# FFN-in with tokens stationary, and two pairs of its blocks per layer as seven products of quadrants

## The chip, the cores and the metric

The kernel runs on one core of a Trainium2 chip. The metric is device microseconds from the start to the end of one execution, smaller is better. The engines of a core are TensorE (PE, with its weight load PEld), VectorE (DVE), ScalarE (ACT), GpSimd (POOL) and SyncE (SP); each runs its own list of instructions in order, and waits in it for semaphores. Transfers are issued from a queue of SP or of GpSimd and run on sixteen DMA engines that all queues share.

## The reference

Two layers, 256 tokens of 1,024 features, everything in 32-bit floats. A layer is a mixer (gated linear attention beside grouped-query attention), then the FFN, then an embedding step:

```python
u = rms_norm(h, g_mix_pre);  h = h + rms_norm(mixed @ w_out, g_mix_post)     # the mixer
gate, up = jnp.split(rms_norm(h, g_ffn_pre) @ w_ffn_in, 2, axis=-1)          # w_ffn_in: 1024 x 5632
h = h + rms_norm((jax.nn.silu(gate) * up) @ w_ffn_out, g_ffn_post)           # w_ffn_out: 2816 x 1024
h = h + rms_norm(jax.nn.sigmoid(h @ w_ple_gate) * (p_i @ w_ple_proj), g_ple_post)
```

The change is in the second line. The hidden width 2,816 is cut into eleven blocks of 256; block b takes 256 gate columns and the 256 up columns that belong to them.

## The kernel before

Every product of 32-bit numbers is made from three products of TensorE in its fp32r type: each operand is split into a rounded high part and the rest, and high x high, high x low and low x high are summed (`mm3`, line 87). The split of one piece is a cast on ScalarE and a subtraction on VectorE (`split`, line 99).

**Weights.** `plan` (line 162) lists, in the order of use, units of 1,024 KB: for FFN-in a unit is 512 rows of one block's 512 columns (`unit_gate_up`), so a block has two, kh = 0 and 1. `Stream` (line 177) takes them through three stages. `load` issues a unit's transfers on SP's queue into one of two `raw` buffers. `fill` splits a unit in two pieces, k = 0, 1 and k = 2, 3, into a pair of buffers `wh` and `wl`, of which there are four, and then issues the next load. `take` hands a split unit to TensorE's code; `done` says that it has been used, and lets `fill` go on. So up to four units are split ahead of their use, the one in use among them.

**Tokens.** `Split` (line 258) holds a matrix in transposed form, features on the partitions and tokens along the free axis, as high and low parts. `u2` is the normed input of the FFN, `hid` its hidden values. `Task` (line 229) is a generator of small work, transposes above all, that `tick` moves on after every few products, so that TensorE meets it some products later; `need` runs it to its end.

**FFN-in** (lines 1027 to 1052). Blocks 0 and 1 have the tokens stationary (`amode`, line 383): 128 tokens by 128 features are loaded, 512 columns of weights move, and the result has tokens on the partitions. One half of the tokens (hf) goes first, since `u2` comes half by half. The gated result is transposed on TensorE (line 291) into `hid`. Blocks 2 to 10 have the weights stationary (`wmode`, line 392): 128 x 128 weights are loaded, 256 tokens move, the result is already transposed, and goes into `hid` after silu and the product with up. FFN-out (from line 1059) reads `hid`.

The order on each engine is fixed when the program is compiled, from the order of the code, priorities and estimated times. Buffers come from pools: `big` has nine of 8 KB a partition, `mid` ten of 4 KB, `acc` and `aux` eight PSUM banks. SCRATCH (1,024 bytes a partition) is what is set aside in SBUF for the descriptors of transfers that GpSimd's queue issues; the kernel before issues none.

Of the kernel before, what the change touches and what calls it, by code (L numbers as in the profile page):

```python
# [9 lines left out]
F32 = mybir.dt.float32  # L10
# [6 lines left out]
P = 128  # L17
T = 256
# [21 lines left out]
def trunk_kernel(ctx: ExitStack, tc: tile.TileContext, a: dict, out: bass.AP):  # L40
# [21 lines left out]
    def nm(s):  # L62
        uid[0] += 1
        return f"{s}_{part[0]}_{uid[0]}"
# [98 lines left out]
    for l in range(DEPTH):  # L163
        w = a["w_in"][l]
        plan += [unit_rows(w, n, C_RA, C_RA + 1056, 2 if l + n == 0 else 1) for n in range(4)]
        for c0 in (C_AK, C_GQ, C_GK, C_GV, C_GV + 512, C_GG, C_GG + 512, C_GA, C_GA + 512, C_GB, C_GB + 512):
            plan += [unit(w, kh, c0) for kh in range(2)]
        for j in range(2):
            for wo in (a["w_o_gla"][l], a["w_o_attn"][l]):
                plan += [unit(wo, kh, j * 512) for kh in range(2)]  # L170
        plan += [unit(a["w_out"][l], kh, j * 512) for kh in range(2) for j in range(2)]
        plan += [unit_rows(a["w_ple_proj"][l], 0)]
        plan += [unit_gate_up(a["w_ffn_in"][l], kh, b) for b in range(NBLK) for kh in range(2)]
        plan += [unit_rows(a["w_ffn_out"][l], n) for n in range(NBLK)]
        plan += [unit(a["w_ple_gate"][l], kh, j * 512) for kh in range(2) for j in range(2)]

    class Stream:


        def __init__(self, depth):  # L180
            self.depth, self.n, self.held, self.raws, self.ready, self.open = depth, 0, 0, [], [], False

        def load(self, between=lambda: None):

            if self.n == len(plan):
                return
            raw = rawp.tile([P, UNIT], F32, tag="raw", name=nm("raw"))
            moves = plan[self.n](raw)
            for dst, src in moves:
                if self.open:  # L190
                    nc.sync.dma_start(dst, src)
                else:
                    on("dma", nc.sync.dma_start, dst, src)
                between()
            self.raws.append((raw, sum(math.prod(dst.shape[1:]) for dst, _ in moves)))
            self.n += 1

        def pieces(self):

            raw, n = self.raws.pop(0)  # L200
# [4 lines left out]
            return [(wh[:, c], wl[:, c], raw[:, c]) for c in (slice(0, n // 2), slice(n // 2, n))]  # L205

        def fill(self):
# [50 lines left out]
    class Split:  # L258


        def __init__(self):
            self.h, self.l = (big(F32R).rearrange("p (k t) -> p k t", t=T) for _ in range(2))
            self.makers = {0: [], 1: []}

        def need(self, hf, k=None):

# [7 lines left out]

        def put(self, src, k, n, t0, tn):

            i = (slice(None), slice(k, k + n), slice(t0, t0 + tn))
            split(self.h[i], self.l[i], src.rearrange("p (k t) -> p k t", t=tn))

        def tok(self, k, hf):  # L280
            s = slice(hf * P, (hf + 1) * P)
            return self.h[:, k, s], self.l[:, k, s]

        def all(self, k):
            return self.h[:, k, :], self.l[:, k, :]

    def transpose_in(sp, src, k, n, hf):

# [103 lines left out]
    def wmode(os_, sp, k0, w, first, last):  # L392
# [9 lines left out]
        for f in range(4):  # L402
# [6 lines left out]
                )  # L409
            tick()  # L410

    def project_t(sp):
# [113 lines left out]
    def turned(hf, k, n):  # L526

        ps = aux()
        for i in range(n):
            on("pe", nc.tensor.transpose, ps[:, i * P : (i + 1) * P], xn[hf][:, (k + i) * P : (k + i + 1) * P], ident)  # L530
        i = (slice(None), slice(k, k + n), slice(hf * P, (hf + 1) * P))
        split_here(uT.h[i], uT.l[i], ps[:, : n * P].rearrange("p (k t) -> p k t", t=P))

    def start():
        square(0, 0)
# [40 lines left out]
    for l in range(DEPTH):  # L576
# [448 lines left out]


        part[0] = f"{l}ffnin"
        hid = [Split() for _ in range(3)]
        us = [[ws.take() for _ in range(2)] for _ in range(2)]
        for hf in range(2):  # L1030
            for b in range(2):
                o = acc()
                for kh in range(2):
                    amode(o, u2, hf, kh * 4, us[b][kh], kh == 0, kh == 1)
                    if hf == 1:
                        ws.done()
                sg = t512()
                nc.scalar.activation(sg[:, 0:256], o[:, 0:256], AF.Silu)
                vmul(sg[:, 0:256], o[:, 256:512], sg[:, 0:256])


                def turn(sg=sg, b=b, hf=hf):
                    yield WAIT_FFN
                    transpose_in(hid[0], sg[:, 0:256], b * 2, 2, hf)

                hid[0].makers[hf].append(Task(turn(), part[0]))
# [17 lines left out]
        def out_step(n, hf, w):  # L1064
            wh, wl = (t[:, :2048].rearrange("p (k c) -> p k c", c=512) for t in w)
            for kk in range(2):
                k = 2 * n + kk
                hid[k // 8].need(hf)
                for j in range(2):
                    mm3(  # L1070
                        o[hf][j], hid[k // 8].tok(k % 8, hf), (wh[:, 2 * kk + j, :], wl[:, 2 * kk + j, :]),
                        k == 0, k == 2 * NBLK - 1,
                    )
                tick()
# [95 lines left out]
```

## Time and profile before

| | |
|---|---|
| median of 3 runs | 953.19 us (952.98 to 954.38) |
| profiled execution | 953.27 us |
| its span, first to last instruction | 951.6 us |
| TensorE busy | 938.7 us, 99% |
| VectorE, ScalarE, GpSimd busy | 612.7, 508.4, 80.9 us |
| granted clock of TensorE | 0.998 |
| read from HBM | 167.41 MB, 177 GB/s over the span |

A row of a group reads: line, engine, operation, output <- inputs by their buffers' names, partitions x elements, count; then busy us and mean ns of one; then the time its engine was idle just before, and what ended that. The number behind a buffer's name is the layer, the text behind it the part of the program in which the buffer was handed out. Products overlap in TensorE, so the mean duration of one is longer than the time from one to the next. In the chain of waits a row is start, length, and what ran (x is the count); "issue" is time in which the engine waited for nothing that the profile shows. A DMA row gives the size of one transfer and the median time from its issue to its landing.

### The profile page before, as it was taken

The numbers are of one execution on the slowest core, as the hardware profiler recorded it, in microseconds if no ns is written. First come the engines' busy times: TensorE is split into PE (matmuls) and PEld (weight loads), VectorE is DVE, ScalarE is ACT, GpSimd is POOL, SyncE is SP. The second block draws the span as 40 slices with busy tenths as digits, with TensorE's granted clock in tenths as the row PEclk, the third lists the DMA queues.
The fourth block names the chain that finished last, engine by engine and source line by source line (L and its number), as shares of the span: only waits on it lengthen the run. The fifth ranks groups of instructions, "written<-read, shape, count | busy, mean of one in ns | idle before, by whom it ended". The sixth has DMA issues, their size and how long they took to land.

```text
span 951.6 us, 13932 instructions
## 1 busy us (share of the span) xinstructions
PE 938.7 (99%) x5561; PEld 836.2 (88%) x5561; DVE 612.7 (64%) x820; ACT 508.4 (53%) x854; POOL 80.9 (8%) x152
## 2 busy tenths in 40 slices
PE   8999999999999999999999999999999999999996
PEld 6998888888889999988889988888888899998886
DVE  4898977456666555545779799664656665555464
ACT  4669676434464544443666686755336554443343
POOL 3400211000120000000132011200001000000000
PEclk9999999999999999999999999999999999999999
DMA  7463444555368655553545515356563676555531
GB/s 239 152 228 126 159 163 148 212 187 198 139 209 288 199 178 178 180 210 121 192 166 178 199 68 188 118 194 208 189 221 131 223 224 191 189 191 180 180 130 44
DMA packets 100766, 169.35 MB, mean 178 GB/s; under 512 B 3735, under 2 KB 51351, under 8 KB 100702
## 3 DMA queue, kind: packets, MB, share of 16 engines
q1 hardware_dynamic: 100702, 168.47, 52.6%
q8 instruction: 43, 0.70, 0.3%
q14 instruction: 21, 0.17, 0.1%
HBM read 167.41 MB, written 1.05 MB: 177 GB/s over the span
## 4 chain that ended last, share of the span: by engine, by line
PE 94%; DVE 1%; POOL 1%; ACT 1%; DMA 1%; issue 1%; SPq 0%; POOLq 0%; DVEq 0%; ACTq 0%
PE acc_0ffnin L85 13%; PE acc_1ffnin L85 13%; PE acc_1ffnout L85 6%; PE acc_0ffnout L85 6%; PE acc_1gate L85 5%; PE acc_0gate L85 5%; PE acc_1merge L85 5%; PE acc_0merge L85 5%; PE acc_1gqk L85 2%; PE acc_0rq L85 2%; PE acc_0gqk L85 2%; PE acc_1wout L85 2%; PE acc_0wout L85 2%; PE acc_1ple L85 2%; PE acc_1gg L85 2%; PE acc_0gg L85 2%
## 5 line engine op out<-in xcount | busy, mean ns | idle before, releaser
L85 PE MATMUL acc_1ffnin<-big_1wout,wh_1ffnin 128*128 128x256 f32 x576 | 103.9, 283 | 0.0
L85 PE MATMUL acc_0ffnin<-big_0wout,wh_0ffnin 128*128 128x256 f32 x576 | 103.9, 283 | 0.0
L85 PEld LDWEIGHTS acc_1ffnin<-big_1wout,wh_1ffnin 128*128 128x128 f32 x576 | 89.8, 192 | 0.0
L85 PEld LDWEIGHTS acc_0ffnin<-big_0wout,wh_0ffnin 128*128 128x128 f32 x576 | 89.8, 192 | 0.0
L85 PE MATMUL acc_1ffnin<-big_1wout,wl_1ffnin 128*128 128x256 f32 x288 | 81.5, 283 | 0.0
L85 PE MATMUL acc_0ffnin<-big_0wout,wl_0ffnin 128*128 128x256 f32 x288 | 81.5, 283 | 0.0
L101 ACT CAST wh_1ffnin<-raw_1ffnin 128x1024 fp32r<-128x1024 f32 x40 | 40.1, 1047 | 52.3 <-PE acc_1ffnin L85 37.9
L97 DVE TENSOR_TENSOR wl_1ffnin<-raw_1ffnin,wh_1ffnin 128x1024 fp32r<-128x1024 f32 x40 | 47.3, 1222 | 31.6 <-ACT wh_1ffnin L101 31.6
L97 DVE TENSOR_TENSOR wl_0ffnin<-raw_0ffnin,wh_0ffnin 128x1024 fp32r<-128x1024 f32 x40 | 47.2, 1222 | 30.0 <-ACT wh_0ffnin L101 30.0
L101 ACT CAST wh_0ffnin<-raw_0ffnin 128x1024 fp32r<-128x1024 f32 x40 | 40.0, 1048 | 48.9 <-PE acc_0ffnin L85 35.5
L85 PEld LDWEIGHTS acc_1ffnin<-big_1wout,wl_1ffnin 128*128 128x128 f32 x288 | 55.3, 192 | 0.0
L85 PEld LDWEIGHTS acc_0ffnin<-big_0wout,wl_0ffnin 128*128 128x128 f32 x288 | 55.3, 192 | 0.0
L85 PE MATMUL acc_0ffnout<-wh_0ffnout,big_0ffnin 128*128 128x512 f32 x112 | 34.9, 390 | 0.0
L85 PE MATMUL acc_1ffnout<-wh_1ffnout,big_1ffnin 128*128 128x512 f32 x112 | 34.9, 390 | 0.0
L97 DVE TENSOR_TENSOR wl_1ffnout<-raw_1ffnout,wh_1ffnout 128x1024 fp32r<-128x1024 f32 x18 | 21.3, 1221 | 18.6 <-ACT wh_1ffnout L101 18.6
L97 DVE TENSOR_TENSOR wl_0ffnout<-raw_0ffnout,wh_0ffnout 128x1024 fp32r<-128x1024 f32 x18 | 21.3, 1221 | 18.4 <-ACT wh_0ffnout L101 18.4
L101 ACT CAST wh_1ffnout<-raw_1ffnout 128x1024 fp32r<-128x1024 f32 x18 | 18.1, 1051 | 24.0 <-PE acc_1ffnout L85 19.8
L101 ACT CAST wh_0ffnout<-raw_0ffnout 128x1024 fp32r<-128x1024 f32 x18 | 18.1, 1051 | 22.6 <-PE acc_0ffnout L85 22.5
L97 DVE TENSOR_TENSOR wl_0gate<-raw_0gate,wh_0gate 128x1024 fp32r<-128x1024 f32 x14 | 16.5, 1222 | 17.8 <-ACT wh_0gate L101 17.8
L97 DVE TENSOR_TENSOR wl_1gate<-raw_1gate,wh_1gate 128x1024 fp32r<-128x1024 f32 x14 | 16.5, 1221 | 17.8 <-ACT wh_1gate L101 17.8
L85 PE MATMUL acc_0rq<-wh_start,big_start 128*128 128x384 f32 (+1 forms) x96 | 25.2, 347 | 1.7 <-ACT big_start L111 1.6
L85 PEld LDWEIGHTS acc_1ffnout<-wh_1ffnout,big_1ffnin 128*128 128x128 f32 x112 | 21.0, 188 | 4.3
(587 smaller groups left out, 2646.0 us busy)
## 6 DMA issues: line engine op xcount, KB each, us to landing
raw_0ffnin<-in_w_ffn_in_dram SPq DMA_DIRECT2D x32, 512.0 KB, 4.0
raw_1ffnin<-in_w_ffn_in_dram SPq DMA_DIRECT2D x32, 512.0 KB, 3.9
raw_0ffnin<-in_w_ffn_out_dram SPq DMA_DIRECT2D x6, 1024.0 KB, 4.8
raw_1ffnin<-in_w_ffn_out_dram SPq DMA_DIRECT2D x6, 1024.0 KB, 5.1
raw_0ffnout<-in_w_ffn_out_dram SPq DMA_DIRECT2D x5, 1024.0 KB, 4.9
raw_1ffnout<-in_w_ffn_out_dram SPq DMA_DIRECT2D x5, 1024.0 KB, 4.8
raw_0rq<-in_w_in_dram SPq DMA_DIRECT2D x4, 1024.0 KB, 4.7
raw_0v<-in_w_in_dram SPq DMA_DIRECT2D x4, 1024.0 KB, 5.0
```

The lines of the kernel that those rows point to most:

```text
L85: return nc.tensor.matmul(o, lhsT, rhs, start=start, stop=stop)
L97: nc.vector.tensor_tensor(out=out, in0=in0, in1=in1, op=ALU.subtract)
L101: nc.scalar.copy(hi, src)
```

## The change

All eleven blocks of FFN-in now have tokens stationary and come out with tokens on the partitions, and each is transposed on TensorE after silu and gating (`turned`). `Split` keeps high and low parts beside each other in buffers of four k, handed out when first used.

Blocks 2, 3 and 6, 7 are two pairs. For a pair the tokens are cut into quadrants A (128 tokens by 512 features: A11 is half 0, features 0 to 511) and the weights into B (B11 and B21 are the two units of the first block, B12 and B22 those of the second). The eight quadrant products of a pair become seven, by Winograd's form of Strassen's scheme:

- sums of A, made once a layer on VectorE (`Forms`): S1 = A21 - A22, S2 = A11 - S1, S3 = A21 - A11, S4 = A12 - S2;
- sums of B: B11 + B12, B22 + B12, B11 + B12 + B22, and that + B21;
- products in this order: A11 B11, S4 B22, S1 (B11 + B12), S3 (B22 + B12), S2 (B11 + B12 + B22), A12 B21, A22 (all four). Five additions or subtractions on VectorE and one copy on ScalarE combine them (`seven`).

B11 and B22 are loaded by SP's queue into buffers of their own (two of `big`), B21 into a `raw` buffer. B12 is never loaded by itself: the sums are made in place, in the own buffers, by transfers of GpSimd's queue that read HBM and add to SBUF (`accum_op`). Each sum is four transfers of 256 KB (gate and up, k in two halves); there are four sums a pair. A sum is issued after the unit that was there has been split, and the next split of that buffer waits for it.

`plan` holds a pair as a list of its four units. `Stream` keeps `loads` and `jobs` apart: a plain unit is one job, a pair seven, and each job is one split unit.

```diff
+PAIRS = (2, 6)
...
+        for b in range(NBLK):
+            us = [unit_gate_up(a["w_ffn_in"][l], kh, b) for kh in range(2)]
+            if b - 1 in PAIRS:
+                plan[-2:] = [[plan[-2], us[0], plan[-1], us[1]]]
+            else:
+                plan += us
...
+            for x in plan:
+                if isinstance(x, list):
+                    self.loads += [(x[0], True), (x[3], True), (x[2], False)]
+                    self.jobs += self.pair(x)
+                else:
+                    self.loads.append((x, False))
+                    self.jobs.append(self.plain())
...
+            self.room += 1
+            while self.n < len(self.loads) and (self.loads[self.n][1] or self.room):
+                make, own = self.loads[self.n]
+                if own:
+                    raw = big()
                 else:
+                    raw = rawp.tile([P, UNIT], F32, tag="raw", name=nm("raw"))
+                    self.room -= 1
...
+        def pair(self, units):
+            b11, b12, b21, b22 = units
+            own = []
+
+            def made(raw, more=None):
+                for piece in self.put(raw, 2048):
+                    split(*piece)
+                if more:
+                    for d, s in more(raw):
+                        for k in (slice(0, 2), slice(2, 4)):
+                            nc.gpsimd.dma_start(d[:, k, :], s[:, k, :], accum_op=ALU.add)
+
+            def step(n, more=None):
+                yield
+                if not own:
+                    own.extend(self.raws.pop(0)[0] for _ in range(2))
+                made(own[n], more)
+
+            def plain():
+                yield
+                made(self.raws.pop(0)[0])
+                self.load()
+
+            return [step(0, b12), step(1, b12), step(0, b22), step(1), step(0, b21), plain(), step(0)]
+
         def fill(self):
-            while self.open and self.held < self.depth and self.raws:
-                for piece in self.pieces():
-                    split(*piece)
-                self.load()
+            while self.open and self.held < self.depth and self.jobs:
+                job = self.jobs.pop(0)
+                next(job)
+                next(job, None)
...
+    class Forms:
...
+        def make(self):
+            yield 1
...
+            for hf in range(2):
+                t = mid().rearrange("p (g k t) -> p g k t", g=2, t=P)
+                for g in range(2):
+                    hi, lo = (p.bitcast(F32) for p in sp.at(4 * g, 4, hf * P, P))
+                    nc.vector.tensor_tensor(out=t[:, g], in0=hi, in1=lo, op=ALU.add)
+                    x[hf, g] = t[:, g]
+            yield 1
+            s1, s2, s3, s4 = x[1, 1], t512().rearrange("p (k t) -> p k t", t=P), x[1, 0], x[0, 1]
+            vsub(s1, x[1, 0], x[1, 1])
+            vsub(s2, x[0, 0], s1)
+            vsub(s3, x[1, 0], x[0, 0])
+            vsub(s4, x[0, 1], s2)
+            self.s = []
+            for f in (s1, s2, s3, s4):
+                parts = [p.rearrange("p (k t) -> p k t", t=P) for p in halves(mid(F32R))]
+                split(*parts, f)
+                self.s.append(parts)
+                yield 1
...
+    def seven(forms):
+        def times(o, f, first=True):
+            wh, wl = (t[:, :2048].rearrange("p (k c) -> p k c", c=512) for t in ws.take())
+            form = forms.get(f)
+            for k in range(4):
+                (fh, fl), h, lo = form(k), wh[:, k, :], wl[:, k, :]
+                for n, (x, y) in enumerate(((fh, h), (fh, lo), (fl, h))):
+                    nc.tensor.matmul(
+                        o, x, y, start=first and k + n == 0, stop=k == 3 and n == 2, skip_group_check=not first
+                    )
+                if k % 2:
+                    tick()
+            ws.done()
...
+        c11, p3, p5, p7, p6 = (acc() for _ in range(5))
+        p1, v = halves(mid())
+        c12, c22 = halves(mid())
+        times(c11, (0, 0))
+        nc.scalar.copy(p1, c11)
+        times(p3, 4)
+        times(p5, 1)
+        times(p7, 3)
+        times(p6, 2)
+        vsub(v, p6, p1)
+        add(v, p5, v)
+        add(c22, p7, v)
+        yield 1, 1, c22
+        add(c12, p3, v)
+        yield 0, 1, c12
+        times(c11, (0, 1), False)
+        yield 0, 0, c11
+        times(p5, (1, 1), False)
+        vsub(v, p5, c22)
+        yield 1, 0, v
...
-        for b in range(2, NBLK):
-            og, ou = project_t(u2)
-            sg = t512()
-            nc.scalar.activation(sg, og, AF.Silu)
-            vmul(sg, ou, sg)
-            hid[b // 4].put(sg, 2 * b % 8, 2, 0, T)
+        forms = Forms(u2)
+        for b in range(2, NBLK):
+            if b in PAIRS:
+                sgs = [t512() for _ in range(2)]
+                for hf, i, o in seven(forms):
+                    gated(sgs[i], hf, o)
+                    turned(sgs[i], b + i, [hf])
+            elif b - 1 not in PAIRS:
                 sg = t512()
+                for hf, o in enumerate(project(u2)):
+                    gated(sg, hf, o)
+                turned(sg, b, [0, 1])
```

`gated` is silu on the gate columns of one half of the tokens and the product with up; `turned` is a task of two or four transposes into one PSUM bank and the split of that bank into `hid`.

More of the change, by code (lines that the diff above doesn't have):

```diff
@@ L261, in __init__, with at @@
         def __init__(self):
-            self.h, self.l = (big(F32R).rearrange("p (k t) -> p k t", t=T) for _ in range(2))
+            self.t = {}
             self.makers = {0: [], 1: []}
+        def at(self, k, n, t0, tn):
+            if k // 4 not in self.t:
+                self.t[k // 4] = big(F32R).rearrange("p (k s t) -> p k s t", s=2, t=T)
+            t = self.t[k // 4]
+            return [t[:, k % 4 : k % 4 + n, s, t0 : t0 + tn] for s in range(2)]
         def need(self, hf, k=None):
@@ L1027, in trunk_kernel, with gated, turned, turn @@
         part[0] = f"{l}ffnin"
-        hid = [Split() for _ in range(3)]
+        hid = Split()
         us = [[ws.take() for _ in range(2)] for _ in range(2)]
+        def gated(sg, hf, o):
+            c = slice(hf * 256, (hf + 1) * 256)
+            nc.scalar.activation(sg[:, c], o[:, 0:256], AF.Silu)
+            vmul(sg[:, c], o[:, 256:512], sg[:, c])
+        def turned(sg, b, halves_):
+            def turn():
+                yield WAIT_FFN
+                n = len(halves_)
+                ps = aux()
+                for k in range(2):
+                    for i, hf in enumerate(halves_):
+                        nc.tensor.transpose(
+                            ps[:, (k * n + i) * P : (k * n + i + 1) * P],
+                            sg[:, hf * 256 + k * P : hf * 256 + (k + 1) * P], ident,
+                        )
+                with tc.high_priority(AHEAD):
+                    hid.put(ps[:, : 2 * n * P], 2 * b, 2, halves_[0] * P, n * P)
+            t = Task(turn(), part[0], 2 * b // 4)
+            for hf in halves_:
+                hid.makers[hf].append(t)
+        sgs = [t512() for _ in range(2)]
         for hf in range(2):
```

69 lines of the change are left out of this document (40 added, 29 removed).

## The prediction

> **What bounds the kernel now.** I read the page from its first part down, then the chain of waits in order of time around FFN-in, then the groups by line, the DMA issues and the timeline. The busy table:
>
> ```profile
> span 951.6 us, 13932 instructions
> PE 938.7 (99%) x5561; PEld 836.2 (88%) x5561; DVE 612.7 (64%) x820; ACT 508.4 (53%) x854; POOL 80.9 (8%) x152
> ...
> q1 hardware_dynamic: 100702, 168.47, 52.6%
> q8 instruction: 43, 0.70, 0.3%
> q14 instruction: 21, 0.17, 0.1%
> ...
> PE 94%; DVE 1%; POOL 1%; ACT 1%; DMA 1%; issue 1%; SPq 0%; POOLq 0%; DVEq 0%; ACTq 0%
> ```
>
> TensorE carries 94% of the chain. No queue of GpSimd appears among the DMA queues, so the one new kind of work in this change, an adding transfer, is not in this trace at all. The pieces of the chain for layer 0 give the rates of both forms of FFN product:
>
> ```profile
> 278.42 5.48 PE acc_0ffnin L85 x24
> 283.90 0.22 PE aux_0ffnin L291 x2
> 284.12 5.46 PE acc_0ffnin L85 x24
> 289.58 0.22 PE aux_0ffnin L291 x2
> 289.80 5.75 PE acc_0ffnin L85 x48
> ```
> ```profile
> 295.76 97.91 PE acc_0ffnin L85 x816
> 393.68 55.79 PE acc_0ffnout L85 x246
> ```
> ```profile
> 449.46 0.87 PE aux_0ffnout L291 x8
> ```
>
> From 289.80 on weights are stationary and 256 tokens move: 97.91/816 = 0.1200 us each. FFN-out has tokens stationary and 512 columns moving: 55.79/246 = 0.2268 us, which is 0.1134 per 256 columns, 5.5% less. A transpose costs 0.87/8 = 0.109 us. In that stretch nothing else is near its limit:
>
> ```profile
> 295.80:393.70 97.90, 97.90 (x817) 97.90 (x816) 52.71 (x53) 43.97 (x54) 0.00 (x0) 1.00 0.64 205
> ```
>
> The columns are TensorE, weight load, VectorE, ScalarE and GpSimd busy, the clock granted, the share of the DMA engines and GB/s. TensorE and the weight load are both full; the DMA engines are at 0.64.
>
> **The change on TensorE.** Per layer, blocks 2 to 10 issue 9 x 96 = 864 products of 256 columns: 864 x 0.1200 = 103.7 us. After it five blocks stay plain, 5 x 48 = 240 products of 512 columns, and two pairs take seven quadrant products of 12 instead of eight, 2 x 84 = 168: 408 x 0.2268 = 92.5 us. Results now come out token-major, so 9 x 4 = 36 transposes are added: 3.9 us. The sum is 96.4, a gain of 7.3 us a layer and 14.6 in two; about 6.2 of each 7.3 is the two pairs, the rest the five blocks. The extra silu and multiply halves and the evictions follow on ScalarE and VectorE, which have room there; if that cover goes, the first to suffer are the transposes, which sit in TensorE's order. Blocks 0 and 1 change nothing.
>
> **The change on the other engines.** Each weight unit of 1,024 columns x 2 is split by these two groups, and the fixed steps of a pair use the third and fourth:
>
> ```profile
> L101 ACT CAST wh_0ffnin<-raw_0ffnin 128x1024 fp32r<-128x1024 f32 x40 | 40.0, 1048 | 48.9 <-PE acc_0ffnin L85 35.5 <-DMA raw_0ffnin<-in_w_ffn_in_dram 13.4
> L97 DVE TENSOR_TENSOR wl_0ffnin<-raw_0ffnin,wh_0ffnin 128x1024 fp32r<-128x1024 f32 x40 | 47.2, 1222 | 30.0 <-ACT wh_0ffnin L101 30.0
> L97 DVE TENSOR_TENSOR big_0ffnin<-t_0ffnin,big_0ffnin 128x512 fp32r<-128x512 f32 x9 | 6.2, 684 | 0.0
> ```
>
> A pair splits seven units instead of four: VectorE 14 x 1.222 = 17.1 us, plus five combinations of products at 0.684 = 3.4 and eight steps of gating and hidden splits, at most 5.5 counted at the same 0.684: up to 26 us against a pair's 84 x 0.2268 + 8 x 0.109 = 19.9 on TensorE. Four units are kept split ahead (9.8 us of VectorE), so one pair alone is covered. The first pair of a layer also makes the four token sums: eight operations and four splits, 12 x 0.684 = 8.2 us of VectorE, and its second product already needs the last of them. I cost this at nothing because the waits below are longer; without them it costs between 0 and 8.2 us a layer.
>
> **The weight sums.** This is the term that decides. Name a unit's sum X: four transfers of 256 KB, issued by GpSimd, which read HBM and what is in SBUF, and write SBUF. A pair has four sums, all in GpSimd's one queue: B12 into B11, B12 into B22, B22 into the first, B21 into the first. Each is queued only after ScalarE and VectorE have split what was there, and the next split waits for it; behind a waiting split stand, in ScalarE's and VectorE's order, later splits, silu and gating. GpSimd computes nothing in that stretch (0.00 above), so the sums are queued behind each other only. SP's queue loads three units a pair instead of four, two of them into large buffers; I cost that at nothing beside DMA engines at 0.64, and at one load, 4.8 us below, if a buffer comes free late. The nearest rows are loads and stores of SP's queue:
>
> ```profile
> raw_0ffnin<-in_w_ffn_in_dram SPq DMA_DIRECT2D x32, 512.0 KB, 4.0
> raw_1ffnin<-in_w_ffn_in_dram SPq DMA_DIRECT2D x32, 512.0 KB, 3.9
> raw_0ffnin<-in_w_ffn_out_dram SPq DMA_DIRECT2D x6, 1024.0 KB, 4.8
> ...
> out_dram<-h SPq DMA_DIRECT2D x3, 256.0 KB, 2.1
> ```
>
> Lower bound: no less than a load of the same 1,024 KB, X = 4.8. Upper bound: the four land one after another, each as slow as a load of the 512 KB that it reads, 4 x 4.0 = 16. From 2.1 at 256 KB to 4.8 at 1,024 KB is 3.5 us per 1,000 KB over a fixed 1.2, so 512 KB in one transfer is 3.0. I take four of these in a row, X = 12, because 1,024 bytes a partition are set aside for the queue's descriptors (SCRATCH) and the code cuts each transfer in two along k, which leaves little room for several in flight; that is a reading of the code, not of a row.
>
> The Trainium skill, page DMA: Bandwidth & Descriptors, section Anatomy of one DMA — SWDGE (gpsimd) path, gives for a transfer of this queue about 2.0 us fixed plus bytes over 436 GB/s, an estimate of 2.6 us for 256 KB that counts no read-back; no row here shows it. Four in a row would be X = 10.4, and the sum below would come to about 1,012 us.
>
> Now the wait. A chain through the first unit runs: half a split (1.048 + 1.222 = 2.3), sum, sum, sum, half a split, sum, half a split, last product (12 x 0.2268 = 2.7): 4X + 9.6. Its cover begins when the split of B11 may start. For the first pair that is the cast here, 8.6 us before TensorE reaches the pair at 289.80:
>
> ```profile
> 281.21 1.05 ACT L101 CAST wh_0ffnin<-raw_0wout 128x1024 fp32r<-128x1024 f32 x1 [2.32 <-PE acc_0ffnin L85]
> ```
>
> So it has 8.6 + 19.9 = 28.5 us. For the second pair, four units ahead means three more units of 24 products (3 x 5.44 = 16.3) and eight transposes (0.9): 37.1 us. At X = 12 the chain is 57.6: TensorE idles 29.1 us in the first pair and 20.5 in the second, 49.6 a layer, 99.2 in two. Against the gain of 14.6 that is +84.6. The profiled execution took 953.27 us, span 951.6 and 1.7 around it; the median of the runs is 953.19, so the sum applies as it is: 953.3 + 84.6 = **1,038 us**. In general the time is 845.9 + 16X while both pairs wait (X over 6.9), and 900.9 + 8X while only the first does (down to 4.7). It breaks even at X = 6.55.
>
> **The rivals.**
> 1. Forecast, one after another: X from 4 x 2.1 = 8.4 to 16, 980 to 1,102 us. For it: one queue, dependent steps, sixteen starts and landings a pair that no other transfer hides. Against it: nothing in the trace shows that transfers of one queue wait for each other; SP's do overlap, as two halves of a unit land in 4.0 each and not 4.0 then 8.0.
> 2. The transfers overlap, but each byte is moved twice, since SBUF is read back. By the slope, 1,024 KB stream in 3.6 us, doubled 7.2, and 1.2 fixed: 8.4 for a sum that must land, 7.2 for one that another follows in the queue. The chain is 2.3 + 8.4 + 7.2 + 7.2 + 2.3 + 8.4 + 2.3 + 2.7 = 40.8; waits 12.3 and 3.7, 32 in two layers: 971 us. Were half the read-back hidden (6.6 and 5.4), the chain would be 33.6 and the time 949. The Trainium skill, page Collectives: The Full Stack, section The bandwidth ceiling: the fold count and why AG ≠ RS ≠ AR, says that an adding transfer issues two read descriptors per chunk and runs at half the rate of a copy; no run here shows it yet. By that rule the 971 holds and not the 949.
> 3. The other side: the sums are hidden. X = 4.8, as a load of the same size; the first pair then waits 0.3 us and the second nothing, 939 us, and up to 8.2 a layer more for the token sums, of which I count 5: 949. It decides below X = 6.55. For it: the DMA engines are a third idle in the stretch. Against: a pair moves seven units where four were moved, in less time, 7 x 1.05 MB in about 28 us, 260 GB/s with no read-back, over the 205 of before.
> A change that does nothing is no rival: the products really fall from 192 to 84 of double width.
>
> **How the numbers follow.** Forecast 0.52, all slower. Rival 2 0.25: 0.20 slower, 0.03 same, 0.02 faster. Rival 3 0.23: 0.21 faster, 0.01 each of the others. Same means within 0.2%, about what a measurement of this kernel can tell. That makes faster 0.23, same 0.04, slower 0.73. The likeliest case's own range is 980 to 1,102; the range for all is 944 to 1,086 (X up to 15), which leaves about one in ten below and one in ten above.
>
> **What would show it.** Per layer, FFN-in's products of 512 columns at 0.227 us with 36 transposes more. Right: in each pair, TensorE idle before its fourth, fifth and seventh product, released by casts or subtractions of own weights, and these by transfers of GpSimd's queue; the second pair of a layer idles some 9 us less than the first; landing of a 256 KB add near 3 us and the next issued after it. Wrong: adds of one sum landing together within 5 to 8 us (rival 2), or no idle before TensorE in the pairs at all, with VectorE's order as the only wait in the first (rival 3). A transfer below 1.6 us in a row of four would also turn the sign.

## Result and the profile after

The changed kernel takes 1,183.07 us (1,179.84 to 1,185.34); the kernel before, on the same chip, 953.31. The ratio is 1.2409, 95% interval 1.2384 to 1.2434. The forecast was 1,038 with a range from 944 to 1,086. So the direction came out, and so did the mechanism (sums that go one after another), but not the size: 230 us slower, not 85.

The profiled execution took 1,179.84 us. Its page, in the same parts as before (busy time, the clock granted in 40 slices, the queue of GpSimd, the chain):

```profile
span 1178.1 us, 12556 instructions
PE 949.0 (81%) x4721; PEld 801.1 (68%) x4721; DVE 669.3 (57%) x914; ACT 542.0 (46%) x916; POOL 164.8 (14%) x216
...
PEclk9999999999558866999999999999985787779999
...
q0 software_dynamic: 17408, 16.78, 10.0%
...
PE 59%; issue 18%; POOL 7%; DMA 7%; DVE 6%; ACT 2%; SPq 0%; POOLq 0%; ACTq 0%; DVEq 0%
```

TensorE carried 94% of the chain and now carries 59%. "issue", GpSimd and DMA had 3% together and now have 32%, most of it the new transfers: their queue is q0, with 17,408 packets for 16.78 MB. The two dips of the clock are the two FFN-in stages. Their windows, layer 0 and 1:

```profile
265.20:505.00 239.80, 132.14 (x553) 105.60 (x552) 101.44 (x124) 79.93 (x113) 46.65 (x45) 0.78 0.55 134
845.10:1086.20 241.10, 132.21 (x553) 105.49 (x552) 99.03 (x122) 78.44 (x110) 39.87 (x34) 0.77 0.54 130
```

All of the loss is here. The same stage of the kernel before, from its first product to FFN-out's first:

```profile
265.90:393.50 127.60, 127.60 (x977) 123.23 (x977) 72.85 (x77) 64.10 (x84) 5.44 (x13) 1.00 0.64 204
733.00:860.20 127.20, 127.20 (x977) 123.08 (x976) 71.54 (x76) 63.16 (x83) 0.86 (x2) 1.00 0.61 197
```

480.9 less 254.8 is 226.1 us, and the two spans differ by 226.5. TensorE is busy for 132.1 us a layer, where 120.1 were expected (127.4 before less 7.3), and waits for the rest. What it waits for in layer 0 (us in total, times, longest):

```profile
PE acc_0ffnin L534 <- ACT mid_0ffnin L103: 50.5, 1, 50.5
PE acc_0ffnin L534 <- DVE mid_0ffnin L542: 27.4, 2, 18.3
PE aux_0ffnin L1198 <- DVE t_0ffnin L96: 22.0, 3, 18.1
PE acc_0ffnin L534 <- ACT wh_0ffnin L103: 6.6, 1, 6.6
PE acc_0ffnin L534 <- DVE wl_0ffnin L99: 1.0, 2, 0.5
```

That is 107.5 us. None of the releasers named is a transfer, so one has to go on to what held those engines. The 50.5 us end with a cast of a token sum on ScalarE (S4, for the second product). ScalarE's own row of time around it:

```profile
294.36 1.05 ACT L103 CAST wh_0ffnin<-big_0wout 128x1024 fp32r<-128x1024 f32 x1 [8.53 <-DMA big_0wout<-in_w_ffn_in_dram]
303.72 1.05 ACT L103 CAST wh_0ffnin<-big_0wout 128x1024 fp32r<-128x1024 f32 x1 [8.32 <-DMA big_0wout<-in_w_ffn_in_dram]
...
341.75 0.61 ACT L103 CAST mid_0ffnin<-mid_0ffnin 128x512 fp32r<-128x512 f32 x1
```

Casts of weights stand ahead of it in ScalarE's fixed order, each waiting some 8 us for two transfers. And GpSimd, which issues them (start, length, then in brackets its idle time before):

```profile
284.34 1.41 POOL L255 DMA_DIRECT2D big_0wout<-in_w_ffn_in_dram  x1 [16.84 <-DVE wl_0ffnin L99]
289.93 1.24 POOL L255 DMA_DIRECT2D big_0wout<-in_w_ffn_in_dram  x1 [4.17 <-issue]
294.52 1.21 POOL L255 DMA_DIRECT2D big_0wout<-in_w_ffn_in_dram  x1 [3.35 <-issue]
...
355.45 1.22 POOL L255 DMA_DIRECT2D big_0wout<-in_w_ffn_in_dram  x1 [3.53 <-issue]
382.00 1.21 POOL L255 DMA_DIRECT2D big_0ffnin<-in_w_ffn_in_dram  x1 [25.33 <-DVE big_0ffnin L99]
...
453.92 1.21 POOL L255 DMA_DIRECT2D big_0ffnin<-in_w_ffn_in_dram  x1 [3.50 <-issue]
```
```profile
big_0wout<-in_w_ffn_in_dram POOLq DMA_DIRECT2D x16, 256.0 KB, 4.4
big_0ffnin<-in_w_ffn_in_dram POOLq DMA_DIRECT2D x16, 256.0 KB, 4.3
```

Each issue takes 1.22 us, each transfer lands 4.4 us after its issue began, and the next begins only then. From the first issue to the last landing the first pair's sixteen adds take 355.45 + 4.4 - 284.34 = 75.5 us, the second's 453.92 + 4.3 - 382.00 = 76.2: 4.7 us each, X = 18.9 and 19.1.

### The profile page after: what moved, and what is told of

Read it like the earlier page. It is cut to its first block, busy times and chain, and to the rows that moved or that the text cites. A ratio compares the mean times of both kernels' runs of the same rounds, so it can differ in the third digit from the quotient of the medians.

```text
span 1178.1 us, 12556 instructions
## 1 busy us (share of the span) xinstructions
PE 949.0 (81%) x4721; PEld 801.1 (68%) x4721; DVE 669.3 (57%) x914; ACT 542.0 (46%) x916; POOL 164.8 (14%) x216
## 3 DMA queue, kind: packets, MB, share of 16 engines
q0 software_dynamic: 17408, 16.78, 10.0%
## 4 chain that ended last, share of the span: by engine, by line
PE 59%; issue 18%; POOL 7%; DMA 7%; DVE 6%; ACT 2%; SPq 0%; POOLq 0%; ACTq 0%; DVEq 0%
PE acc_0ffnout L87 5%; PE acc_1ffnout L87 5%; PE acc_0ffnin L87 4%; PE acc_1gate L87 4%; PE acc_0gate L87 4%; PE acc_1merge L87 4%; PE acc_0merge L87 4%; PE acc_1ffnin L87 2%; PE acc_1gqk L87 2%; PE acc_0gqk L87 2%; PE acc_1ple L87 2%; PE acc_0gg L87 2%; PE acc_1gg L87 2%; PE acc_0rq L87 2%; PE acc_1v L87 2%
## 5 line engine op out<-in xcount | busy, mean ns | idle before, releaser
L534 PE MATMUL acc_1ffnin<-wh_1ffnin,mid_1ffnin 128*128 128x512 f32 x64 | 24.9, 464 | 57.9 <-ACT mid_1ffnin L103 51.3
L534 PE MATMUL acc_0ffnin<-wh_0ffnin,mid_0ffnin 128*128 128x512 f32 x64 | 24.9, 464 | 57.1 <-ACT mid_0ffnin L103 50.5
L534 PEld LDWEIGHTS acc_1ffnin<-wh_1ffnin,mid_1ffnin 128*128 128x128 f32 x64 | 14.6, 230 | 62.0 <-ACT mid_1ffnin L103 51.7
L534 PEld LDWEIGHTS acc_0ffnin<-wh_0ffnin,mid_0ffnin 128*128 128x128 f32 x64 | 14.6, 230 | 61.2 <-ACT mid_0ffnin L103 51.0
L87 PE MATMUL acc_1ffnin<-wh_1ffnin,big_1wout 128*128 128x512 f32 x160 | 51.5, 395 | 0.0
L87 PE MATMUL acc_0ffnin<-wh_0ffnin,big_0wout 128*128 128x512 f32 x160 | 51.4, 395 | 0.0
L99 DVE TENSOR_TENSOR wl_1ffnin<-big_1ffnin,wh_1ffnin 128x1024 fp32r<-128x1024 f32 x12 | 14.6, 1224 | 61.8 <-ACT wh_1ffnin L103 61.8
L99 DVE TENSOR_TENSOR wl_0ffnin<-big_0ffnin,wh_0ffnin 128x1024 fp32r<-128x1024 f32 x12 | 14.6, 1224 | 61.6 <-ACT wh_0ffnin L103 61.6
L99 DVE TENSOR_TENSOR wl_1ffnin<-big_1wout,wh_1ffnin 128x1024 fp32r<-128x1024 f32 x12 | 14.5, 1223 | 54.6 <-ACT wh_1ffnin L103 54.6
L99 DVE TENSOR_TENSOR wl_0ffnin<-big_0wout,wh_0ffnin 128x1024 fp32r<-128x1024 f32 x12 | 14.5, 1224 | 53.9 <-ACT wh_0ffnin L103 53.9
L534 PE MATMUL acc_0ffnin<-wh_0ffnin,big_0wout 128*128 128x512 f32 x48 | 18.8, 456 | 27.4 <-DVE mid_0ffnin L542 27.4
L534 PE MATMUL acc_1ffnin<-wh_1ffnin,big_1wout 128*128 128x512 f32 x48 | 18.7, 454 | 27.3 <-DVE mid_1ffnin L542 27.3
L99 DVE TENSOR_TENSOR wl_0ffnin<-raw_0ffnin,wh_0ffnin 128x1024 fp32r<-128x1024 f32 x28 | 33.6, 1229 | 11.7 <-ACT wh_0ffnin L103 11.6
L103 ACT CAST wh_1ffnin<-raw_1ffnin 128x1024 fp32r<-128x1024 f32 x28 | 28.5, 1048 | 17.2 <-PE acc_1ffnin L87 8.8
L103 ACT CAST wh_0ffnin<-raw_0ffnin 128x1024 fp32r<-128x1024 f32 x28 | 28.3, 1049 | 13.1 <-PE acc_0ffnin L87 9.2
```

What stands on the lines that cost most here:

```text
L87: return nc.tensor.matmul(o, lhsT, rhs, start=start, stop=stop)
L99: nc.vector.tensor_tensor(out=out, in0=in0, in1=in1, op=ALU.subtract)
L103: nc.scalar.copy(hi, src)
L534: nc.tensor.matmul(o, x, y, start=first and k + n == 0, stop=k == 3 and n == 2, skip_group_check=not first)
```

## Experiments

Theory R: the adds go one at a time for lack of room for their descriptors. Rival S: GpSimd's queue, or the adding itself, is serial whatever the room. Theories on what is left without the sums come after. The kernels of e4, e7, e9 to e12, e14 and e18 leave the weight sums out, those of e10, e12 and e14 the token sums too: their times price a part of the change and are not times of the whole computation.

### e1: token-major alone

```diff
-PAIRS = (2, 6)
+PAIRS = ()
```

> No pairs: FFN-in token-major in all blocks, no sums, no transfers of GpSimd's queue. Both theories: the loss is all in the pairs, so this is before less 18 blocks x (96 x 0.1200 - 48 x 0.2268 - 4 x 0.109 = 0.2 us) = 953.3 - 3.6 = about 950 us; a token-major form that costs by itself would be over 955.

Measured: 950.97 us, ratio 0.9982 (0.9974 to 0.9991). Its FFN-in of layer 0:

```profile
263.30:389.70 126.40, 125.52 (x577) 103.62 (x576) 80.72 (x98) 66.51 (x95) 10.37 (x13) 1.00 0.65 205
```
```profile
PE aux_0ffnin L1198 <- DVE t_0ffnin L96: 0.9, 1, 0.9
```

TensorE's busy time falls by 1.9 us a layer; by the prediction's rates nine blocks give 103.7 - (432 x 0.2268 + 36 x 0.109) = 1.8. Of that, 0.9 goes to one wait at a transpose. So the loss is wholly in the pairs: without them the kernel is 0.2% faster than before.

### e2: room for more descriptors

```diff
-SCRATCH = 1024
+SCRATCH = 1792
```

> 768 bytes a partition more for the descriptors of GpSimd's queue (1,792 instead of 1,024), nothing else. Theory R (room: one adding transfer's descriptors fill over half of the 1,024 bytes, so the next is not written until it has landed): several are in flight, a sum of four falls from 18.7 us to about 8, bound by 1.22 us of issue each, and the kernel to 970 to 1,020 us. Theory S (an adding transfer holds the queue until it has landed, whatever the room): 1,183 us as after.

Measured: 1,019.81 us, ratio 1.0703 (1.0685 to 1.0722).

```profile
283.06 3.90 POOL L255 DMA_DIRECT2D big_0wout<-in_w_ffn_in_dram  x3 [17.11 <-DVE wl_0ffnin L99]
288.63 1.22 POOL L255 DMA_DIRECT2D big_0wout<-in_w_ffn_in_dram  x1 [1.67 <-issue]
```

With 75% more room three adds are issued without a pause, and the waits between later ones are mostly near 1 us or under. One constant takes away 163 of the 230 us. That is R; by S the time would have stayed at 1,183.

### e3: adds of half the size

```diff
-                        for k in (slice(0, 2), slice(2, 4)):
+                        for k in (slice(0, 1), slice(1, 2), slice(2, 3), slice(3, 4)):
```

> The same sums in eight transfers of 128 KB instead of four of 256 KB, room 1,024 bytes. Theory R: two or three are in flight, each costs about its issue, 8 x 1.22 = 10 us and a landing a sum: X near 12, about 1,040 us. Theory S: eight turns of issue and landing, at least 8 x 3.5 = 28 us a sum, 1,290 us or more.

Measured: 1,067.36 us, ratio 1.1202 (1.1178 to 1.1227), 27 us over what was expected. Twice as many transfers, and 116 us faster than the changed kernel:

```profile
283.90 2.90 POOL L255 DMA_DIRECT2D big_0wout<-in_w_ffn_in_dram  x3 [17.96 <-DVE wl_0ffnin L99]
```
```profile
q0 software_dynamic: 18432, 16.79, 11.2%
```

Three of 128 KB are issued in a row where one of 256 KB was. That is R again; by S it would have been slower. The packets would give an estimate of the room: 17,408/64 = 272 for an add of 256 KB, 18,432/128 = 144 for one of 128 KB. In 1,024 bytes a partition 3 x 144 = 432 went and 2 x 272 = 544 did not; in 1,792 bytes 3 x 272 = 816 did. But e4 does not fit this estimate, as its rows show.

### e4: the same transfers without adding

The transfers overwrite, so the weight sums are left out.

```diff
-                            nc.gpsimd.dma_start(d[:, k, :], s[:, k, :], accum_op=ALU.add)
+                            nc.gpsimd.dma_start(d[:, k, :], s[:, k, :])
```

> The same transfers on GpSimd's queue, but they overwrite instead of adding, so the weight sums are left out. Theory R with the read-back as the cause of the long descriptor lists: half the descriptors, so two or three are in flight, a sum of about 7 us, 955 to 985 us. Theory R without it, or theory S for every transfer of this queue: the turn stays near 4 us, 1,100 to 1,183 us. Theory S for adding transfers alone: 955 to 985 us too.

Measured: 991.43 us, ratio 1.0405 (1.0382 to 1.0428), a little above what was expected.

```profile
q0 software_dynamic: 5120, 16.78, 5.6%
```
```profile
big_0wout<-in_w_ffn_in_dram POOLq DMA_DIRECT2D x16, 256.0 KB, 3.5
```

The same bytes need 80 packets a transfer and not 272, and 5.6% of 991.7 us of DMA time instead of 10.0% of 1,178.1: 55.5 against 117.8, 2.1 times less. So an add costs double on the DMA engines. The Trainium skill says the same of the adding step of collectives (page Collectives: The Full Stack, section The bandwidth ceiling: the fold count and why AG ≠ RS ≠ AR); the trace agrees, with 2.1. But most of the loss is not this double cost: e2 makes the same adds and is 163 us faster.

```profile
290.96 2.17 POOL L255 DMA_DIRECT2D big_0wout<-in_w_ffn_in_dram  x3 [2.68 <-issue]
```

After its first three transfers GpSimd pauses here too, for 2.68 us, although four would be 4 x 80 = 320 packets and 432 went in e3. In e2, e3 and e4 alike three are issued in a row at the start. So either packets are not what fills the room, or three in flight is a limit of its own; no run tells these apart. What e2 and e3 do show is that the room is why only one add of 256 KB was in flight.

### e5, e6, e8: the order of the pair, with the small and the larger room

The token sums are made before the first pair, and the seventh product gets a PSUM bank of its own, so that no product waits for a combination:

```diff
         forms = Forms(u2)
+        forms.task.need()
...
-        times(p5, (1, 1), False)
-        vsub(v, p5, c22)
+        p8 = acc()
+        times(p8, (1, 1))
+        add(v, p8, v)
```

(`vsub(v, p5, c22)` moves ahead of the sixth product.) e6 adds room 1,792 to it, e8 also `PAIRS = (4, 8)`.

> Room 1,024 as after; two orders changed: the token sums are made and split before the pairs begin, and the seventh product has a PSUM bank of its own, so it no longer waits for VectorE's combinations, which stand behind splits. Theory C (the chain of sixteen adds sets the time, the 50 us before the second product only show where it is felt): 16 turns of 4.66 are 74.6 a pair, 9.6 around them, covers 28.5 and 37.1; about 1,145 us, the rest of after's 1,183 being order. Theory O (the order of ScalarE and VectorE is the main cause): below 1,050 us.

> e5's order with the room of 1,792 bytes. Theory C: with three adds in flight the last of a pair landed 35 us (first pair) and 39 to 44 us (second) after its first cast, plus half a split and a product of 2.7: waits of 12 and 7 us a layer, 953 - 14.6 + 38 = about 977 us. If the two orders are worth nothing: 1,020 as with the room alone.

> As e6 with the pairs at blocks 4, 5 and 8, 9, so that both have three plain units ahead. Theory C: both pairs wait as the second of e6, 4 x 7 us in all, against 953 - 14.6: about 967 us. If it is the number of adds and not the cover that counts: as e6.

Measured: e5 1,192.39 us, ratio 1.2515 (1.2487 to 1.2543); e6 1,026.9, 1.0780 (1.0752 to 1.0807); e8 1,022.07, 1.0729 (1.0707 to 1.0751). None came near what the better order was expected to give. In e5 the 50.5 us before the second product are gone, but of the 107.5 us of waits in layer 0 98.4 are left, most of them in

```profile
PE aux_0ffnin L1200 <- DVE t_0ffnin L96: 47.3, 7, 18.7
PE acc_0ffnin L534 <- ACT wh_0ffnin L103: 41.2, 9, 8.6
```

The chain of sums is as long as before, so the wait comes up at the next things in TensorE's order. And where there was one long wait there are now many short ones, with slower products after them (the rows of e10 below show such products): TensorE is busy for 978.1 us in all, not 949.0, and that is more than the waits gave back. A wait that a trace names need not be worth its length.

### e7, e9, e10, e11: what is left when nothing is added

e7 is e5 with the transfers on SP's queue, overwriting; e9 has no transfers at all; e10 leaves out the token sums too; e11 is e7 with the pairs at blocks 4 and 8.

```diff
-                            nc.gpsimd.dma_start(d[:, k, :], s[:, k, :], accum_op=ALU.add)
+                            nc.sync.dma_start(d[:, k, :], s[:, k, :])
```

> e5's order; the sixteen transfers a pair are issued by SP's queue and overwrite instead of adding, so the weight sums are left out and no descriptor is made by GpSimd. Theory C: a unit of 1,024 KB lands in about 5 us, the chain of 4 x 5 + 9.6 fits into the cover, about 940 to 945 us: the seven products' whole gain. Theory V (VectorE is full in the pairs, seven units split for seven products): 950 us or more.

> The kernel of e7 (token sums made ahead of the first pair, seventh product in a PSUM bank of its own), with the 32 in-place transfers a layer left out altogether: the own units are split again as they are, so the weight sums are left out, and 3 units a pair are read from HBM and not 7. What is left of the pairs is TensorE's seven products and the work of VectorE and ScalarE. In e7 FFN-in lasted 137.1 us a layer; the token-major kernel of e1 needs 126.3, and two pairs should take 10.9/2 = 5.4 off that: 120.9. So 16.2 us a layer are to be explained. Theory V (VectorE and ScalarE: 102.7 us of VectorE a layer in e7 against 80.7 in e1, in an order that lets the transposes and the next weights wait): the transfers are not the reason, 960 to 975. Theory D (the transfers: DMA engines at 0.74 to 1.03, loads of the next weights late): FFN-in falls to about 121, 940 to 945.

> As e9, and the four token sums of a layer are left out as well (eight operations and four splits; the products of the pairs take quadrants of the tokens as they are). This prices what the prediction costed at nothing, bounded by 8.2 us a layer. Theory V: 8 us a layer faster than e9 or more, since the sums stand in VectorE's order ahead of the first pair's weight splits, 942 to 955. Theory D: within 3 us of e9, since VectorE has room in both. If e9 and e10 are both above 955, it is the seven splits of a pair (17.1 us of VectorE) and not the token sums.

> The kernel of e7 (transfers overwrite, on SP's queue, so the weight sums are left out) with the pairs moved from blocks 2-3 and 6-7 to 4-5 and 8-9, so that both are preceded by plain blocks and the token sums have a plain block's time to spare. Theory V: VectorE catches up before each pair, so the first pair loses less: 960 to 970. Theory D: the bytes are the same wherever the pairs stand, 972 to 976. If 945 or less, the seven products do pay once they are far enough from the stage's start.

Measured: e7 974.11 us, ratio 1.0220 (1.0198 to 1.0243); e9 963.38, 1.0106 (1.0089 to 1.0122); e10 959.61, 1.0068 (1.0049 to 1.0088); e11 964.58, 1.0121 (1.0106 to 1.0136). So even with nothing to add the pairs lost, and theory D (the transfers) explains only 11 of the 34 us between e7 and the 940 of seven products (the sum of the prediction, and e14 below), the token sums 4. The times of e7, e9 and e11 lie where theory V put them, that of e10 does not; e14 shows that VectorE's load was not the reason. In e10 what TensorE waits for in the pairs of layer 0, and rows of its timeline and of its chain:

```profile
PE aux_0ffnin L1195 <- DVE t_0ffnin L96: 5.6, 4, 2.4
```
```profile
309.98 0.44 PE L1195 MATMUL aux_0ffnin<-ident,t_0ffnin 128*128 128x128 f32 x2 [0.56 <-DVE t_0ffnin L96]
312.48 0.66 PE L1195 MATMUL aux_0ffnin<-ident,t_0ffnin 128*128 128x128 f32 x2 [2.07 <-DVE t_0ffnin L96]
...
313.37 0.63 PE L87 MATMUL acc_0ffnin<-wl_0ffnin,big_0wout 128*128 128x512 f32 x1
313.80 1.05 PE L87 MATMUL acc_0ffnin<-wh_0ffnin,big_0wout 128*128 128x512 f32 x2
```
```profile
313.15 4.09 PE acc_0ffnin L87 x12
```

All waits in the pairs are at transposes, which stand two products behind the gating whose result they turn. And the products behind the second of these waits are slow: they start 0.43 us apart, where 0.2268 is the rate of the prediction, and twelve take 4.09 us.

### e12, e13: a third raw buffer

```diff
-    rawp = ctx.enter_context(tc.tile_pool(name="rawp", bufs=2))
+    rawp = ctx.enter_context(tc.tile_pool(name="rawp", bufs=3))
-    b4p = ctx.enter_context(tc.tile_pool(name="b4p", bufs=10))
+    b4p = ctx.enter_context(tc.tile_pool(name="b4p", bufs=8))
```

> The kernel of e10 (no in-place transfers, no token sums, so both are left out of the computation) with three buffers for raw weight units and not two; the pool of the 4 KB tiles shrinks from 10 to 8 to make room. Theory L (the units behind a pair are loaded too late: in e10 a load is issued only after the pair's plain unit is split, and its cast comes 5 us later, with a silu and so the transposes behind it): the waits of the transposes (5.6 and 6.1 us a layer) and the half clock after them go, FFN-in from 130.5 to about 121 to 124 us a layer, 942 to 948. Theory B (the bunched work of a pair on VectorE and ScalarE): 957 to 961, as e10. FFN-in's length is what counts, since the smaller pool may cost something elsewhere.

> The token-major kernel of e1 (no pairs, the whole computation) with the same three raw buffers and 8 tiles of 4 KB. FFN-in is already bound by TensorE there (126.3 us a layer, 125.4 of them busy), so by both theories it stays at 126 and the time at 951, give or take 2 us for the smaller pool. A larger change would mean that e12 has to be read against this kernel.

Measured: e12 956.96 us, ratio 1.0041 (1.0020 to 1.0063); e13 950.53, 0.9975 (0.9965 to 0.9984). In e12 FFN-in, from its first product to FFN-out's first, is 128.0 us a layer instead of 130.7: late loads were a small part. Not every wait costs TensorE its clock. The two pairs of layer 0:

```profile
311.33 0.83 PE L1195 MATMUL aux_0ffnin<-ident,t_0ffnin 128*128 128x128 f32 x4 [2.70 <-DVE t_0ffnin L96]
...
357.46 0.82 PE L1195 MATMUL aux_0ffnin<-ident,t_0ffnin 128*128 128x128 f32 x4 [2.98 <-DVE t_0ffnin L96]
```
```profile
312.16 2.76 PE acc_0ffnin L87 x12
...
358.28 4.27 PE acc_0ffnin L87 x12
```

After a wait of 2.70 us twelve products take 2.76 us, after one of 2.98 they take 4.27. That is no threshold: in layer 1 it is the longer wait, 2.90 us, that is followed by 2.76, and the shorter, 2.83, by 4.34; and in e10 one of 2.07 us, close behind one of 0.56, was enough. What decides it beside the length, these traces do not show.

### e14, e15, e16: the transposes later in TensorE's order

`WAIT_FFN` is the number of ticks (two a product of 12) after which `turned`'s transposes enter TensorE's order. e14 is e10, e15 is e2, e16 is e1 (with 6 ticks):

```diff
-WAIT, WAIT_FIRST, WAIT_NEXT, WAIT_H, WAIT_FFN, WAIT_MIX = 6, 4, 9, 5, 4, 3
+WAIT, WAIT_FIRST, WAIT_NEXT, WAIT_H, WAIT_FFN, WAIT_MIX = 6, 4, 9, 5, 10, 3
```

> The kernel of e10 (no in-place transfers and no token sums, so both are left out of the computation), with FFN-in's transposes put ten ticks (five products of 12, about 13.6 us) after their task is made instead of four (5.4 us): WAIT_FFN 10. If only the place of the transposes costs (theory P), TensorE no longer waits 5.6 to 6.1 us a layer at them, the half clock after these waits goes too, FFN-in falls from 130.5 to 121 to 124 us a layer, 940 to 948. If VectorE and ScalarE are short of time in and after a pair (theory B), the wait moves to the products that need the next split weights, 955 to 961.

> The whole computation: the kernel of e2 (room for three adds, 1,792 bytes, median 1,019.8) with WAIT_FFN 10. In e2 TensorE waits 19.0 us a layer before its second product for the token sums' split, 13.1 before combinations, only 2.2 at transposes. So by either theory little goes: 1,012 to 1,020. If 1,000 or less, the transposes hold up more than their own wait shows.

> The whole computation without pairs: the kernel of e1 (median 950.97) with WAIT_FFN 6, that is transposes three products after the gating. TensorE waits 0.9 us a layer at one transpose in e1; by theory P this goes, 949 to 950; if VectorE is late there for another reason, 951.

Measured: e14 940.19 us, ratio 0.9870 (0.9851 to 0.9888); e15 1,018.17, 1.0665 (1.0639 to 1.0690); e16 951.05, 0.9976 (0.9965 to 0.9986). e14 settles it for the pairs without sums: one number moves 19 us, FFN-in has no wait left,

```profile
265.70:385.20 119.50, 119.50 (x549) 98.71 (x548) 94.49 (x112) 76.74 (x108) 7.53 (x13) 1.00 0.59 188
```

and VectorE, at 94.5 of 119.5 us, was not short of time. Theory B is out. e16 missed: its FFN-in is 125.4 us a layer against 126.5 in e1, but the whole kernel is no faster than e1.

### e17, e18: all of it together

e17 is e8 with WAIT_FFN 10, the whole computation; e18 is e11 with it.

> The whole computation, with everything mended that the runs priced: room for three adds (1,792 bytes), token sums ahead of the pairs, seventh product in a PSUM bank of its own, pairs at blocks 4-5 and 8-9 (the kernel of e8, 1,022.1), and now the transposes ten ticks back. Adds come every 2.07 us in e2 (12 in 24.9 us), so a sum of four takes 8.3, the chain through a pair's first unit 4 x 8.3 + 9.6 = 42.8 us against a cover of 37.1 for either pair: 5.7 us of waiting a pair, 22.8 in all. With the 940.2 of e14 and the 3.8 of the token sums: 967. Theory X (the chain of the sums is what is left): 960 to 975. If the transposes' place costs nothing beside the sums, as in e15: 1,010 to 1,022. Break-even with the kernel before would be 953.

> The kernel of e11 (transfers overwrite, on SP's queue, so the weight sums are left out; token sums early, pairs at 4-5 and 8-9; 964.6) with the transposes ten ticks back. Against e14 it has the token sums and the 32 transfers a layer in addition. If the place of the transposes was the whole loss there too, FFN-in has no wait and the time is 940 to 945; if the transfers hold up the splits for themselves, 950 or more.

Measured: e17 996.63 us, ratio 1.0454 (1.0428 to 1.0480); e18 939.63, 0.9862 (0.9846 to 0.9878). FFN-in of layer 0 of e18 and of e17, and what TensorE waits for in e17:

```profile
265.10:385.30 120.20, 119.89 (x550) 98.81 (x549) 97.50 (x119) 75.91 (x110) 6.44 (x10) 1.00 0.77 249
```
```profile
266.30:415.10 148.80, 131.63 (x550) 102.12 (x549) 96.26 (x116) 74.76 (x105) 43.62 (x37) 0.94 0.82 197
```
```profile
PE acc_0ffnin L534 <- ACT wh_0ffnin L103: 10.2, 6, 2.9
PE acc_0ffnin L534 <- DVE wl_0ffnin L99: 6.5, 11, 0.8
```

e18 makes the token sums, splits seven units a pair and moves all the bytes, and TensorE is busy for 119.89 of 120.20 us. So in e17 the adds, on GpSimd's queue, cost 57 us against plain transfers on SP's: in layer 0 16.7 us of waits and 11.7 of slower products. What of this is the adding and what the queue, no run separates. The expected 967 missed by 30. The chain of waits has the adds of the two pairs from

```profile
299.75 3.90 POOL big_0ffnin L255 x3
...
335.30 6.84 DMA big_0ffnin<-in_w_ffn_in_dram
...
362.77 1.44 POOL big_0ffnin L255 x2
...
390.90 7.12 DMA big_0ffnin<-in_w_ffn_in_dram
```

299.75 to 342.1 and 362.77 to 398.0, so X is 10.6 and 8.8 and not 8.3, and the slower clock was not in the expected sum.

Of the kernels that do the whole computation, the token-major ones without pairs are the fastest (e1, e13, e16: 950.5 to 951.1); they beat the kernel before by 0.2%, and no version with pairs that adds the weights did.

## Why the prediction was wrong

**The term that was mis-sized: X.** The mechanism was as put, sums one after another in GpSimd's queue, and for the reason that was read from the code: the room for descriptors (e2, e3). But "four in a row, each 3.0 us" measured 4.7 us, X = 18.9 and not 12, above even the upper bound of 16. That bound took a load of SP's queue as the slowest an add could be. It left out two things: GpSimd itself spends 1.22 us on each issue, which with one in flight lies on the path, and an add makes 2.1 times the work of a plain transfer of the same bytes (e4). How the 1.7 us between 3.0 and 4.7 divide between these, no run shows. A price taken from another queue and another kind of transfer is no upper bound.

**The chain held in the changed kernel.** Put X = 18.9 and 19.1 into 4X + 9.6 and take off the covers of 28.5 and 37.1: 56.7 and 48.9, 105.6 us of waits a layer. Measured: 107.5 in layer 0, 108.8 in layer 1. The sum would have been 953.3 - 14.6 + 211.2 = 1,150. With faster sums the chain was no longer all of it: X = 8.3 gives 20.0 us a layer, and e2 waits for 34.3. What the changed kernel's sum still lacked is the next term.

**The clock.** TensorE is busy for 132.1 us a layer instead of the 119.9 of e18: after each long wait its products run at about half speed for some microseconds (0.43 us apart in e10). In the chain of the changed kernel:

```profile
368.29 4.74 PE acc_0ffnin L534 x12
...
471.18 2.76 PE acc_0ffnin L87 x12
```

That is 12 us a layer, 24 in all, which no step of the prediction counted; it brings the sum to 1,174 of 1,180; the 5 us more that were measured in the waits are nearly all the rest.

**Costed at nothing.** Token sums, combinations, gating, the extra splits and SP's loads: e18 has all of them and runs at 939.6, the 939 of rival 3 before the 5 us a layer that it counted for the token sums. So they can be hidden: there with the token sums made early, the pairs at blocks 4 and 8, and the transposes far enough back. With the transposes four ticks back they were not: "the first to suffer are the transposes, which sit in TensorE's order" named the place, at no price. The price was 19 us in e10 and 25 in e11. In the changed kernel it lies under the waits for the sums; e5 and e15 show that little is gained there by one change of order, and e17 against e8 that 25 us are gained once the others are made too.

**Signs.** Right: the next add issued after the last had landed; the second pair idling less than the first (50.5 and 27.4 - 18.3 = 9.1 in the first, 59.6 together, the other 47.9 in the second: 11.7 less, 9 predicted). Wrong: the landing near 3 us, and the places. In the first pair TensorE stopped before the second product, not before the fourth and fifth (the stop before the seventh was there, 9.0 us), because the cast of S4 came behind the weights' casts on ScalarE: the step that let the token sums hide beneath longer waits overlooked that the waiting casts were queued ahead of them.

**Rivals.** Rival 2's rate, 8.4 us a sum, is about what e2 shows (8.3, worked out in the expectation of e17), but at the price of 67 us over the kernel before and not 18. Its sum had 16.0 us of waits a layer; e2 has 19.0 before the second product, 13.1 before combinations and 2.2 at transposes, and 12.0 us of slower products in both layers together (125.8 us busy a layer in place of 119.9). The largest wait ends again with the cast of S4. Rival 3's 939 was the right time for hidden sums, and no run with sums came near it.

## What to carry to other kernels

Before many transfers are queued on GpSimd, find out how many can be in flight in the room set aside for their descriptors; the sign in a trace that one fills it is an issue that begins only when the transfer before it has landed, and a larger room or smaller transfers are cheap trials. When a fixed order holds waits, price them by taking the cause away: removing the wait that the trace named gained nothing in e5, while moving the transposes back by three products gained 19 us in e14. And add to a forecast wait the slower products that can follow it: 12 us a layer here, beside 107.5 of waiting.

## What was not expected of the hardware

- Issuing an add of 256 KB holds GpSimd for 1.22 us, and three plain transfers of that size take 2.41 us, 0.8 each (e4):

```profile
285.87 2.41 POOL L255 DMA_DIRECT2D big_0wout<-in_w_ffn_in_dram  x3 [16.92 <-DVE wl_0ffnin L99]
```

- An add needs 272 packets for 256 KB, a plain transfer 80, and twice the time on the DMA engines.
- TensorE's products ran at about half speed after waits of 2.98 and 2.83 us, and not after 2.70 and 2.90 (e12), so the length of the wait alone does not decide it. The Trainium skill, page TensorE: Matmul & The Clock Gate, section Part 1: The HAM clock gate (the "warmup" mystery), puts the return to half rate at one idle window or more, about 3.4 us; here shorter waits were sometimes enough.
